# Stores to scratch memory on GpSimd's queue, loads and the final output on SyncE's

## The chip, the cores and the metric

The kernel runs on one core of a Trainium2 chip. The metric is the device time of one execution in microseconds (us), here the median of several. The engines of the core are TensorE (PE in the rows, PEld for its weight loads), VectorE (DVE), ScalarE (ACT), GpSimd (POOL) and SyncE (SP). Each works through its own instructions in order and waits for the others by semaphores. A transfer between the chip's memory and SBUF (a DMA) is issued as an instruction of one engine and then runs by itself. SPq in a row is SyncE's queue of such issues.

## What is computed

The reference is a trunk of two layers over 512 latent tokens and 256 context tokens, 1024 wide, in float32. Each layer modulates its input, projects it into three groups of heads (a state-space scan, latent attention, retention), gates each group, joins them, projects back and normalises:

```python
h_l = x * (1 + sc_l) + sh_l
parts_l = jnp.split(h_l @ w_in, in_splits(), axis=-1)
ssd_l, ssd_c = ssd_mixer(parts_c[0:3], parts_l[0:3], ...)
mla_l, mla_c = mla_mixer(parts_c[3:7], parts_l[3:7], ...)
ret_l, ret_c = retention_mixer(parts_c[7:11], parts_l[7:11], ...)
out_l = jnp.concatenate([ssd_l, mla_l, ret_l], -1) @ w_out
x_new = layer_norm(ALPHA * x + g_l * out_l, ln_g, ln_b)
```

The same is done for the context tokens (`_c`) in layer 0; in layer 1 only latent tokens go on. The latent attention first projects low-rank vectors into queries, keys and values, then attends with eight heads over all 768 tokens.

## The kernel before

Everything is held transposed, features on the 128 partitions and tokens along the row; 1024 features are eight tiles. A float32 product is made of three products of a reduced float32 format: ScalarE casts an operand to its high part (`wh` from the raw weight `wr`), VectorE subtracts it to get the low part (`wl`), and `mm3` (the helper around `mm`, L101) issues high x high, high x low and low x high. Raw weights of 512 KB come through two `wr` buffers, their two parts through three `wh` and `wl` buffers each. Outputs of a projection collect in accumulators named `pj` or `po`.

What does not fit in SBUF goes to scratch tiles in the chip's memory and is read back later, in every stage:

- `store` spills projections through a staging ring of three tiles `st`; `xbc` stores the convolved `xs`; `ssd_y` the scan's output `y`; `dt_stage` the small `kr` and `cum`.
- `ret_v` stages retention values in two buffers `stv` on the way to `rv`; `ret_y` stores the retention output to the scratch tiles `m4` to `m7`.
- `mla_prep` makes the attention's operands. All its results go through one ring of two buffers, tag `st`: the keys `kn` (four stores a layer), the values `v` (six, tile name `stv`), the queries `qh` (16). A buffer can be written again when its store has landed. Scores of one key head read `qr`, `kr` and `vr`, which are loaded back from `qh`, `kn`, `krr` and `v`; GpSimd's memsets (L991 to L994) fill the constant rows of those operands.
- `mla_head` normalises two heads at a time: the sums `den` are stored to `dd`, loaded back as `dc` spread over 128 partitions, inverted, stored to `de` and loaded back as `den`; then VectorE multiplies `num` by it and stores to `m0` to `m2`. This is done three times a layer.
- `out_s` runs half of the output projection beside the attention: it loads the residual `ox`, takes the accumulator `po` through VectorE's `oy`, adds, and stores to the scratch tile `a`. The loads `mraw` bring the retention output back, and ScalarE and VectorE split it into its two parts `mr`.
- `ln` stores the layer's output `x` and a row `rr`, to be read in the next layer.

Between these, `tick` spreads the modulation matmuls (`pr`, weights `ar`) over the program.

In the kernel before, all loads and all stores are `self.load`, that is `nc.sync.dma_start`, so SyncE issues them all, in one order. The order of each engine is set by a scheduler from the program's order, priorities (`high_priority` around the staging copies) and a cost of each instruction of its own.

Of the kernel before, what the change touches and what calls it, by code (L numbers as in the profile page):

```python
# [88 lines left out]
class Trunk:  # L89
# [7 lines left out]
    def load(self, out, in_):  # L97
        return self.nc.sync.dma_start(out=out, in_=in_)

# [331 lines left out]
    def dt_stage(self):  # L431
# [26 lines left out]
        self.load(D["kr"], ms[0:32, :])  # L458
# [50 lines left out]
        for d, m in ((0, self.mf), (1, self.mb)):  # L509
# [8 lines left out]
            self.load(D["cum"][d].rearrange("c h i -> h c i"), ct.rearrange("h (c i) -> h c i", i=128))  # L518
# [32 lines left out]
    def xbc(self, g):  # L551
# [8 lines left out]
        for t in range(4):  # L560
            u = self.conv(X_T + g * 4 + t)
            if self.ctx:
                self.load(D["xs"][g * 4 + t][:, 0:NCTX], u[:, 0:NCTX])
            self.load(D["xs"][g * 4 + t][:, NCTX:T], u[:, 260:XC])
# [42 lines left out]
    def ssd_y(self, c, g, hf, hb):  # L607
# [50 lines left out]
        self.load(D["y"][g][:, :, c * 128:(c + 1) * 128].rearrange("t p i -> p t i"), ys)  # L658


    def ret_v(self):
        l = self.l
        for n in range(2):
            sl = [self.wslot(self.A["win"][l, RV_T + n * 2 + j]) for j in range(2)]
            sl = [(a.rearrange("p (k c) -> p k c", k=4), b.rearrange("p (k c) -> p k c", k=4)) for a, b in sl]
            for c in range(NCH):
# [4 lines left out]
                with self.tc.high_priority():  # L671
# [9 lines left out]
                    self.load(self.D["rv"][:, c, n * 256:(n + 1) * 256], st)  # L681
# [145 lines left out]
    def ret_y(self, P, c0, q, kk, v, Dm, ef, hs):  # L827
# [44 lines left out]
        for s in range(2):  # L872
# [6 lines left out]
            for pr in range(2):  # L879
                self.load(D["m"][4 + pr * 2 + s][:, cs], gt[:, s, pr])  # L880


    def mla_prep(self, P):
# [47 lines left out]
        self.load(D["krr"], ko)  # L931
# [5 lines left out]
        for p in range(4):  # L937
# [7 lines left out]
            self.load(D["kn"][p], st)  # L945
        wvh, wvl = v3(wv[0], 2), v3(wv[1], 2)
        for c in range(NCH):
# [5 lines left out]
            self.load(D["v"][:, c, :], st)  # L953
# [3 lines left out]
        for s in (2, 0, 1):  # L957
            w = self.pslot(P, self.A["wuq"][l, s], 768)
            wh, wl = v3(w[0][:, 0:768], 3), v3(w[1][:, 0:768], 3)
            for j in range(2):  # L960
# [13 lines left out]
                if ti < 4:  # L974
                    for s2 in range(2):
                        self.load(D["qh"][ti * 2 + s2][0:64, lo:], st[64 * s2:64 * s2 + 64, lo:])
                else:
                    for s2 in range(4):
                        self.load(D["qh"][(ti - 4) * 4 + s2][64:96, lo:], st[32 * s2:32 * s2 + 32, lo:])
# [63 lines left out]
    def mla_head(self, P, h):  # L1043
# [37 lines left out]
        for i in range(2):  # L1081
            self.load(d1[i:i + 1, :], den[64 * i:64 * i + 1, lo:])
# [3 lines left out]
        self.load(fl(d2), dc)  # L1086
# [4 lines left out]
        self.load(D["m"][p][:, lo:], num[:, lo:])  # L1091
# [47 lines left out]
    def out_s(self, t):  # L1139
# [17 lines left out]
        self.load(self.D["a"][t][:, lo:], x[:, lo:])  # L1157
# [88 lines left out]
    def ln(self, P, X, a, b, qsum, xsum):  # L1246
# [32 lines left out]
        for t in range(8):  # L1279
# [5 lines left out]
            if a >= NCTX:  # L1285

                self.load(D["x"][t][:, a:b], X[t])
        if a >= NCTX:
            rr = P.tile([1, NLAT], F32, name="rr")
            self.copy(rr, pb[0:1, :])  # L1290
            self.load(self.rrd, rr)
# [91 lines left out]
```

## Time and profile before

| | us |
|---|---|
| median of 3 runs (1486.96 to 1489.88) | 1487.89 |
| the profiled execution | 1487.2 |
| its span | 1485.4 |
| TensorE busy (share of the span) | 1418.2 (95%) |
| VectorE busy | 1084.7 (73%) |
| ScalarE busy | 693.0 (47%) |
| GpSimd busy | 22.5 (2%) |

The profile records one execution. Its span runs from the first to the last instruction, and the rest of the execution's time, 1.8 us, lies around it. Issues of transfers, waits and register work are not counted as busy. A busy TensorE is not one at its peak, since matmuls overlap and their ends are modelled. A row such as "PE po <- DVE oy" tells that TensorE stood idle before the instruction that writes `po`, and that VectorE's instruction on `oy` ended the wait.

### The profile page before, as it was taken

The page shows a single profiled execution, that of the slowest core. Times are in us where ns is not written, and L with a number is a line of the kernel's source. Part 1 is how long each engine was busy: PE and PEld are TensorE (multiplying, and loading weights), DVE is VectorE, ACT ScalarE, POOL GpSimd, SP SyncE. Part 2 cuts the span into 40 slices and gives each one's busy share as a digit, 9 for nine tenths or more (in the row PEclk, how much of TensorE's full clock was granted, in tenths as well). Part 3 has the DMA queues.
Part 4 walks back from the last instruction along what each step waited for, and adds up shares of the span by engine and source line. Part 5 has one row for each costly group of instructions (what it writes and reads, how often), then busy time and mean ns, then how long its engine had stood idle before and what let it go on. Part 6 is the DMA issues. An engine that isn't in the chain of part 4 may idle for free. (4 is left out here: it accounts for less than half of the span.)

```text
span 1485.4 us, 23355 instructions
## 1 busy us (share of the span) xinstructions
PE 1418.2 (95%) x8660; PEld 1158.9 (78%) x8660; DVE 1084.7 (73%) x2132; ACT 693.0 (47%) x1376; POOL 22.5 (2%) x31
## 2 busy tenths in 40 slices
PE   6999999999999999999999799999999999989996
PEld 4787789778888878777788688789878887767665
DVE  3599894995485657678745858998697678678858
ACT  2346743662232434477721245565363335347743
POOL 0000000000000001000001000000000000000010
PEclk9999999999999999999999899999999999999998
DMA  8336543457724746724242222353257455563241
GB/s 335 137 101 178 184 171 107 158 183 256 256 72 157 254 160 182 240 65 137 89 156 71 91 88 87 129 135 114 86 171 226 173 188 189 196 202 98 67 128 57
DMA packets 110155, 225.66 MB, mean 152 GB/s; under 512 B 13581, under 2 KB 42381, under 8 KB 109786
## 3 DMA queue, kind: packets, MB, share of 16 engines
q1 hardware_dynamic: 110042, 224.17, 46.2%
q8 instruction: 68, 1.11, 0.3%
q14 instruction: 45, 0.37, 0.1%
HBM read 173.93 MB, written 50.20 MB: 151 GB/s over the span
## 5 line engine op out<-in xcount | busy, mean ns | idle before, releaser
L101 PE MATMUL pj<-hh,wh 128*128 128x512 f32 (+1 forms) x984 | 354.6, 361 | 2.0 <-ACT hh L115 1.6
L101 PE MATMUL pj<-hh,wl 128*128 128x512 f32 (+1 forms) x984 | 352.7, 359 | 0.0
L101 PE MATMUL pj<-hl,wh 128*128 128x512 f32 (+1 forms) x984 | 349.9, 356 | 0.0
L122 ACT CAST wh<-wr 128x1024 fp32r<-128x1024 f32 (+1 forms) x116 | 120.3, 1039 | 207.1 <-PE pj L101 94.0
L101 PEld LDWEIGHTS pj<-hh,wh 128*128 128x128 f32 x984 | 186.7, 190 | 34.0 <-issue 9.3
L101 PEld LDWEIGHTS pj<-hh,wl 128*128 128x128 f32 x984 | 186.4, 190 | 29.4 <-issue 7.0
L101 PEld LDWEIGHTS pj<-hl,wh 128*128 128x128 f32 x984 | 186.7, 190 | 29.0 <-issue 6.4
L104 DVE TENSOR_TENSOR wl<-wr,wh 128x1024 fp32r<-128x1024 f32 (+1 forms) x116 | 142.4, 1227 | 75.8 <-ACT wh L122 75.0
L104 DVE TENSOR_TENSOR pel<-pe,peh 128x512 fp32r<-128x512 f32 (+1 forms) x112 | 71.6, 648 | 35.8 <-ACT peh L115 35.3
L107 DVE SCALAR_TENSOR_TENSOR cv<-xpad,cw,cv 128x772 f32<-128x772 f32 (+1 forms) x96 | 92.2, 994 | 0.2
L115 ACT ACTIVATE pe<-psc 128x512 f32<-128x512 f32 (+1 forms) x112 | 63.7, 569 | 55.6 <-PE psc L101 46.7
L1035 DVE TENSOR_REDUCE nm<-pmx 128x1 fp32r<-128x768 f32 (+1 forms) x80 | 67.6, 845 | 15.8 <-PE pmx L101 14.6
L101 PE MATMUL po<-sh,wh 128*128 128x512 f32 (+1 forms) x192 | 69.4, 364 | 4.2 <-DVE oy L107 4.2
L101 PE MATMUL po<-sl,wh 128*128 128x512 f32 (+1 forms) x192 | 69.5, 363 | 1.7 <-DVE sl L107 1.7
L115 ACT ACTIVATE ce<-cf 64x512 f32<-64x512 f32 (+1 forms) x80 | 46.9, 586 | 49.6 <-DMA cf<-cum 48.9
L101 PE MATMUL po<-sh,wl 128*128 128x512 f32 (+1 forms) x192 | 68.9, 360 | 0.0
L115 ACT ACTIVATE tm<-sf,dt 128x128 f32<-128x128 f32 x160 | 52.5, 390 | 30.2 <-DVE sf L104 30.2
L115 ACT ACTIVATE peh<-psc 128x512 fp32r<-128x512 f32 (+1 forms) x112 | 63.6, 568 | 0.2
L115 ACT ACTIVATE arg<-arg,ncb 128x128 f32<-128x128 f32 x160 | 54.9, 393 | 4.2 <-DVE arg L107 3.8
L101 PE MATMUL pv<-wl,hh 128*128 128x256 f32 x192 | 54.7, 285 | 0.3 <-DVE wl L104 0.3
L101 PE MATMUL po<-mr,wh 128*128 128x256 f32 (+1 forms) x216 | 54.8, 339 | 0.0
L101 PE MATMUL pv<-wh,hl 128*128 128x256 f32 x192 | 54.5, 284 | 0.0
(330 smaller groups left out, 2952.2 us busy)
## 6 DMA issues: line engine op xcount, KB each, us to landing
wr<-in_win SPq DMA_DIRECT2D x82, 512.0 KB, 3.8
ar<-in_wada SPq DMA_DIRECT2D x48, 512.0 KB, 7.0
cf<-cum SPq DMA_DIRECT2D x80, 256.0 KB, 4.6
wr<-in_wout SPq DMA_DIRECT2D x32, 512.0 KB, 4.0
y<-ys SPq DMA_DIRECT2D x20, 256.0 KB, 2.6
xs<-th SPq DMA_DIRECT2D x16, 256.0 KB, 2.1
x<-in_xT SPq DMA_DIRECT2D x8, 384.0 KB, 8.7
rv<-stv SPq DMA_DIRECT2D x24, 128.0 KB, 2.6
```

The costliest lines, as they stand in the source:

```text
L101: return self.nc.tensor.matmul(out, lhsT=lhsT, rhs=rhs, start=start, stop=stop, **k)
L104: return self.nc.vector.tensor_tensor(out, a, b, op=op)
L107: return self.nc.vector.scalar_tensor_tensor(out, in0=a, scalar=s, in1=b, op0=op0, op1=op1)
L115: return self.nc.scalar.activation(out, in_, f, **k)
L122: self.nc.scalar.copy(hi, raw)
L1035: nc.vector.tensor_reduce(nm[:, i:i + 1], p1[:, 0:n], axis=AX.X, op=ALU.max, negate=True)
```

## The change

A new method `save` issues a transfer from GpSimd instead of SyncE, and every store to a scratch tile uses it: in `store`, `dt_stage`, `xbc`, `ssd_y`, `ret_v`, `ret_y`, `mla_prep`, `mla_head`, `out_s` and `ln`, some 230 stores. Loads and the store of the final output stay on SyncE. Source lines of the changed kernel are four higher (`mm` is L105 instead of L101).

```diff
     def load(self, out, in_):
         return self.nc.sync.dma_start(out=out, in_=in_)
 
+    def save(self, out, in_):
+
+        return self.nc.gpsimd.dma_start(out=out, in_=in_)
+
...
-            self.load(dst[:, ps[-1][1]:T], st[:, ps[-1][1]:T])
+            self.save(dst[:, ps[-1][1]:T], st[:, ps[-1][1]:T])
...
-                    self.load(self.D["rv"][:, c, n * 256:(n + 1) * 256], st)
+                    self.save(self.D["rv"][:, c, n * 256:(n + 1) * 256], st)
...
-            self.load(D["kn"][p], st)
+            self.save(D["kn"][p], st)
...
-            self.load(D["v"][:, c, :], st)
+            self.save(D["v"][:, c, :], st)
...
-                        self.load(D["qh"][ti * 2 + s2][0:64, lo:], st[64 * s2:64 * s2 + 64, lo:])
+                        self.save(D["qh"][ti * 2 + s2][0:64, lo:], st[64 * s2:64 * s2 + 64, lo:])
...
-            self.load(d1[i:i + 1, :], den[64 * i:64 * i + 1, lo:])
+            self.save(d1[i:i + 1, :], den[64 * i:64 * i + 1, lo:])
         dc = P.tile([128, k], F32, tag="dc", name="dc", bufs=2)
         self.load(dc, fl(d1))
         nc.vector.reciprocal(dc, dc)
-        self.load(fl(d2), dc)
+        self.save(fl(d2), dc)
...
-        self.load(self.D["a"][t][:, lo:], x[:, lo:])
+        self.save(self.D["a"][t][:, lo:], x[:, lo:])
```

The other stores are changed in the same way. Since the scheduler places every instruction anew, the order of the other engines changes in many small places too. Names below carry the number of the buffer.

SyncE, before, at the end of the query projections of layer 1 (`m5_1` to `m7_1` are retention scratch, `x3_0` is layer 0's output):

```order
L98 DMA mraw_13142<-m5_1_8742 128x512
L98 DMA qh2_1_8725<-st_12417 64x512
L98 DMA qh3_1_8726<-st_12417 64x512
L98 DMA qh4_1_8727<-st_12437 64x512
L98 DMA wr_14284<-in_wout 128x1024
L98 DMA qh5_1_8728<-st_12437 64x512
L98 DMA qh6_1_8729<-st_12451 64x512
L98 DMA qh7_1_8730<-st_12451 64x512
L98 DMA mraw_13146<-m6_1_8743 128x512
L98 DMA mraw_13150<-m7_1_8744 128x512
L98 DMA ox_14015<-x3_0_620 128x512
L98 DMA qr_12868<-qh0_1_8723 96x512
```

SyncE, after, the same place:

```order
L98 DMA wr_14140<-in_wout 128x1024
L98 DMA mraw_13138<-m4_1_8741 128x512
L98 DMA mraw_13142<-m5_1_8742 128x512
L98 DMA mraw_13146<-m6_1_8743 128x512
L98 DMA mraw_13150<-m7_1_8744 128x512
L98 DMA ox_14015<-x3_0_620 128x512
L98 DMA wr_14252<-in_wout 128x1024
L98 DMA ox_14054<-x4_0_621 128x512
L98 DMA qr_12868<-qh0_1_8723 96x512
```

The query stores have left this order, the four `mraw` loads stand next to each other, and `wr_14284` no longer stands ahead of the last two of them and of `qr`.

VectorE, before, where the first half of the output projection meets the start of attention in layer 1 (`st` are query stagings, `identr` a constant of the attention):

```order
L104 TENSOR_TENSOR wl_14143<-wr_14140,wh_14142 128x1024
L104 TENSOR_TENSOR mr11_12834<-mraw_13142,mr01_12830 128x512
L104 TENSOR_TENSOR st_12451<-pq_12452,nrb_12320 128x512
L104 TENSOR_TENSOR wl_14255<-wr_14252,wh_14254 128x1024
L984 CAST identr_12846<-K_72 128x128
L104 TENSOR_TENSOR mr12_12835<-mraw_13146,mr02_12831 128x512
L107 SCALAR_TENSOR_TENSOR oy_14016<-po_13990,mod1_77,rsb_12765 128x512
```

VectorE, after, the same place:

```order
L108 TENSOR_TENSOR wl_14104<-wr_14101,wh_14103 128x1024
L108 TENSOR_TENSOR mr12_12835<-mraw_13146,mr02_12831 128x512
L111 SCALAR_TENSOR_TENSOR oy_14016<-po_13990,mod1_77,rsb_12765 128x512
L108 TENSOR_TENSOR st_12451<-pq_12452,nrb_12320 128x512
L108 TENSOR_TENSOR mr13_12836<-mraw_13150,mr03_12832 128x512
L111 SCALAR_TENSOR_TENSOR ox_14015<-ox_14015,ag_552,rsb_12765 128x256
L111 SCALAR_TENSOR_TENSOR ox_14015<-ox_14015,ag_552,m3_12837 128x256
L111 SCALAR_TENSOR_TENSOR ox_14015<-ox_14015,ag_552,oy_14016 128x512
L111 SCALAR_TENSOR_TENSOR oy_14055<-po_14029,mod1_77,rsb_12765 128x512
L111 SCALAR_TENSOR_TENSOR ox_14054<-ox_14054,ag_552,rsb_12765 128x256
L108 TENSOR_TENSOR wl_14143<-wr_14140,wh_14142 128x1024
L988 CAST identr_12846<-K_72 128x128
```

`oy_14016` stood behind `wl_14255` and now stands ahead of `wl_14143`, which comes before that; `mr12` is ahead of it in both.

TensorE, before, at the start of attention in layer 0 (`pnm` turns the row maxima round, `pmx` are scores for maxima, `psc` scores):

```order
L101 MATMUL po_7541<-sh7_5885,wl_7513 128x256
L101 MATMUL pnm_6235<-identr_5962,nm_6212 1x128 x2
L101 MATMUL pnm_6239<-identr_5962,nm_6212 1x128 x4
L101 MATMUL pmx_6257<-bkh1_5976,bqh1_5974 128x256
L101 MATMUL psc_6292<-bqh0_5964,bkh0_5966 128x512
```

TensorE, after, the same place:

```order
L105 MATMUL po_7541<-sh7_5885,wl_7513 128x256
L105 MATMUL pnm_6235<-identr_5962,nm_6212 1x128 x2
L105 MATMUL pnm_6239<-identr_5962,nm_6212 1x128 x4
L105 MATMUL pr_7566<-ar_7567,sil_78 32x128 x8
L105 MATMUL pmx_6257<-bkh1_5976,bqh1_5974 128x256
L105 MATMUL psc_6292<-bqh0_5964,bkh0_5966 128x512
```

Eight modulation matmuls `pr` now stand between `pnm` and `pmx`.

## Rows read from the trace of the kernel before

**Rows 1.** The page: busy time, share of the span and instructions of each engine.

```profile
PE 1418.2 (95%) x8660; PEld 1158.9 (78%) x8660; DVE 1084.7 (73%) x2132; ACT 693.0 (47%) x1376; POOL 22.5 (2%) x31
```

**Rows 2.** What TensorE waited for: us in total, times, longest us.

```profile
PE prs L101 <- DVE rs_y L107: 10.5, 3, 4.7
...
PE po L101 <- DVE oy L107: 4.2, 2, 3.7
...
PE pq L101 <- ACT stv L115: 1.7, 1, 1.7
...
PE pvv L101 <- ACT stv L115: 1.3, 1, 1.3
```

**Rows 3.** What SyncE's queue waited for, same columns.

```profile
SPq L98 <- DVE wl L104: 239.6, 66, 12.1
...
SPq L98 <- ACT stv L115: 62.6, 35, 5.0
...
SPq L98 <- DVE ox L107: 46.6, 11, 21.1
```

**Rows 4.** Timeline of SyncE, layer 1: start, length, instruction, [idle before].

```profile
1300.47 0.34 SPq L98 DMA_DIRECT2D wr<-in_wout  x1
1300.87 1.92 SPq L98 DMA_DIRECT2D qh<-st  x3
...
1304.47 0.43 SPq L98 DMA_DIRECT2D qr<-qh  x1
...
1312.32 0.34 SPq L98 DMA_DIRECT2D a<-ox  x1
```

**Rows 5.** Timeline of VectorE, same place.

```profile
1306.77 1.23 DVE L104 TENSOR_TENSOR wl<-wr,wh 128x1024 fp32r<-128x1024 f32 x1 [5.12 <-ACT wh L122]
...
1308.77 0.75 DVE L107 SCALAR_TENSOR_TENSOR oy<-po,mod,rsb 128x512 f32<-128x512 f32 x1
```

**Rows 6.** Timeline of TensorE, start of attention, layer 0 and layer 1.

```profile
612.05 0.40 PE L101 MATMUL pnm<-identr,nm 128*1 128x128 f32 x4 [1.67 <-ACT bqh L118]
613.12 0.58 PE L101 MATMUL pmx<-bkh,bqh 96*128 96x256 f32 x1 [0.66 <-ACT bqh L118]
...
1309.57 0.79 PE L101 MATMUL po<-sh,wh 128*128 128x512 f32 x1 [3.69 <-DVE oy L107]
...
1325.14 0.40 PE L101 MATMUL psc<-bqh,bkh 97*128 97x512 f32 x1
```

**Rows 7.** Stretches: window, busy us and instructions by engine, granted clock, DMA share, GB/s.

```profile
610.00:620.00 10.00, 7.57 (x24) 5.16 (x25) 6.56 (x10) 4.72 (x8) 0.00 (x0) 0.66 0.75 270
...
1310.00:1320.00 10.00, 8.70 (x33) 6.47 (x33) 7.97 (x13) 4.06 (x6) 0.00 (x0) 0.87 0.80 238
```

**Rows 8.** The page, DMA issues: count, KB each, median us from issue to landing.

```profile
kn<-st SPq DMA_DIRECT2D x8, 384.0 KB, 2.3
v<-stv SPq DMA_DIRECT2D x12, 256.0 KB, 5.9
```

**Rows 9.** GpSimd's instructions by line: count, busy us, mean ns, idle before.

```profile
L1214 POOL TENSOR_TENSOR lxs<-lxs,la 128x512 f32<-128x512 f32 (+1 forms) x6 | 7.5, 1253 | 15.4 <-issue 10.3 <-DVE la L107 4.9
...
L991 POOL MEMSET bql<- 1x768 f32 x4 | 3.0, 741 | 677.8 <-DVE yg L104 677.7
```

**Rows 10.** What ScalarE waited for: us in total, times, longest us.

```profile
ACT stv L115 <- DMA rv<-stv: 6.4, 2, 3.7
...
ACT stv L115 <- DMA v<-stv: 5.1, 4, 1.8
```

**Rows 11.** What VectorE waited for, same columns.

```profile
DVE st L104 <- DMA qh<-st: 2.0, 2, 1.1
...
DVE num L107 <- DMA den<-de: 0.6, 1, 0.6
```

**Rows 12.** Timeline of SyncE, one of the six denominator chains.

```profile
725.60 0.32 SPq L98 DMA_DIRECT2D de<-dc  x1
727.00 1.09 SPq L98 DMA_DIRECT2D den<-de  x2
```

More of the change, by code (lines that the diff above doesn't have):

```diff
@@ L457, in dt_stage @@
                 self.padded[t] = self.pad(self.pre[t])
-        self.load(D["kr"], ms[0:32, :])
+        self.save(D["kr"], ms[0:32, :])
         pt = self.ps("tr", "pt", 2)
@@ L517, in dt_stage @@
             self.copy(ct[:, 512:T], pb[0:16, 0:256])
-            self.load(D["cum"][d].rearrange("c h i -> h c i"), ct.rearrange("h (c i) -> h c i", i=128))
+            self.save(D["cum"][d].rearrange("c h i -> h c i"), ct.rearrange("h (c i) -> h c i", i=128))
         self.cw = S.tile([128, 72], F32, name="cw")
@@ L562, in xbc @@
             if self.ctx:
-                self.load(D["xs"][g * 4 + t][:, 0:NCTX], u[:, 0:NCTX])
-            self.load(D["xs"][g * 4 + t][:, NCTX:T], u[:, 260:XC])
+                self.save(D["xs"][g * 4 + t][:, 0:NCTX], u[:, 0:NCTX])
+            self.save(D["xs"][g * 4 + t][:, NCTX:T], u[:, 260:XC])
             self.trans(u, self.xt[:, :, t * 128:(t + 1) * 128])
@@ L657, in ssd_y @@
         self.tt(yv, cv[hs[0][0]], py, ALU.add)
-        self.load(D["y"][g][:, :, c * 128:(c + 1) * 128].rearrange("t p i -> p t i"), ys)
+        self.save(D["y"][g][:, :, c * 128:(c + 1) * 128].rearrange("t p i -> p t i"), ys)
     def ret_v(self):
@@ L879, in ret_y @@
             for pr in range(2):
-                self.load(D["m"][4 + pr * 2 + s][:, cs], gt[:, s, pr])
+                self.save(D["m"][4 + pr * 2 + s][:, cs], gt[:, s, pr])
     def mla_prep(self, P):
@@ L930, in mla_prep @@
         nc.vector.tensor_copy(ko[:, 0:NCTX], kr[:, 0:NCTX])
-        self.load(D["krr"], ko)
+        self.save(D["krr"], ko)
         wk = self.pslot(P, self.A["wukv"][l, 0], 1024)
@@ L975, in mla_prep @@
                     for s2 in range(2):
-                        self.load(D["qh"][ti * 2 + s2][0:64, lo:], st[64 * s2:64 * s2 + 64, lo:])
+                        self.save(D["qh"][ti * 2 + s2][0:64, lo:], st[64 * s2:64 * s2 + 64, lo:])
                 else:
                     for s2 in range(4):
-                        self.load(D["qh"][(ti - 4) * 4 + s2][64:96, lo:], st[32 * s2:32 * s2 + 32, lo:])
+                        self.save(D["qh"][(ti - 4) * 4 + s2][64:96, lo:], st[32 * s2:32 * s2 + 32, lo:])
     def mla(self, P):
@@ L1090, in mla_head @@
         self.tt(num[:, lo:], num[:, lo:], gt[:, lo:], ALU.mult)
-        self.load(D["m"][p][:, lo:], num[:, lo:])
+        self.save(D["m"][p][:, lo:], num[:, lo:])
     def mla_last(self, P):
@@ L1285, in ln @@
             if a >= NCTX:
-                self.load(D["x"][t][:, a:b], X[t])
+                self.save(D["x"][t][:, a:b], X[t])
         if a >= NCTX:
@@ L1290, in ln @@
             self.copy(rr, pb[0:1, :])
-            self.load(self.rrd, rr)
+            self.save(self.rrd, rr)
 INS = ["xT", "cT", "wada", "win", "wuq", "wukv", "wout", "pc", "cpack", "rope"]
```

## The prediction

> **What bounds the kernel now.** The first view is the busy time of the engines [rows 1]: TensorE is busy for 95% of the span, so about 67 us of the 1485.4 are not matmul, and no change of queues can win more than a part of those. The second is the list of what TensorE waited for [rows 2]. Its largest entry is a chain of small VectorE operations, `rs_y`, that no store touches. The entries that a store can move are three: 4.2 us for `oy` (3.7 of it once), 1.7 and 1.3 us for `stv`, the staging tile of a store. The third view is what SyncE's queue waited for [rows 3]: it stood 239.6 us for `wl`, the release of a weight buffer, and 62.6 and 46.6 us for store sources, `stv` and `ox`. All of it is in program order, so a load behind a store waits until the store's source is written, and a store behind a weight load waits until that buffer is free. These long waits cost nothing where the loads run far enough ahead; the holes of TensorE tell where they do not.
>
> **The change, part by part.** The profiled execution took 1487.2 us, span 1485.4 and 1.8 around it; the median of the three runs is 1487.89, 0.7 us above it. The sum is made against 1487.2. A measurement of this kernel can tell about 0.2%, 3.0 us, so faster means below 1484.9 and slower above 1490.9.
>
> *The start of attention in layer 1.* Here TensorE has its one long hole that the change reaches: `po` starts at 1309.57 after 3.69 us without work, and waits for `oy` [rows 6]. `oy` frees the accumulator. On VectorE it stands behind `wl`, which starts at 1306.77 after 5.12 us for ScalarE's `wh` [rows 5], and that operand belongs to a weight that SyncE could only fetch at 1300.47, with three query stores behind it; the first head's query load follows at 1304.47 [rows 4]. The changed order takes all query stores out of SyncE and puts the four `mraw` loads in one block. As a result the scheduler places `oy` ahead of that `wl`: it now stands behind `mr12` instead. If nothing else is late, all 3.69 us go. What is next late is `mr12` itself, which needs a `mraw` load and a ScalarE cast, and one earlier weight operand. I take half, -1.85; ends -3.69 and 0.
>
> *The start of attention in layer 0.* Two holes, 1.67 and 0.66 us, both waiting for the cast `bqh` [rows 6]. The first stays: ScalarE's order before that cast is the same in both kernels, with a weight cast ahead of it. Ahead of the second, eight modulation matmuls (`pr`) now stand between `pnm` and `pmx`, which fill it: -0.66; ends -0.66 and 0.
>
> *The value stores of the latent attention.* The 12 stores `v<-stv` take 5.9 us from issue to landing where the larger `kn<-st` take 2.3 [rows 8], and with two staging buffers ScalarE waited 5.1 us in four places for them [rows 10]. Both of TensorE's holes behind `stv` [rows 2] come from this, 1.7 + 1.3 = 3.0 us. In before, such a store is issued into the same queue as the 512 KB weight loads. In a queue that holds stores alone it may land as `kn` does: -3.0. Or it lands as late as now and is issued later by GpSimd: the cost of that is not in the trace, since GpSimd issues no data there. Its lower bound is the 3.6 us (5.9 - 2.3) that a store can gain. For the upper I take the nearest work that GpSimd does: a memset of 741 ns and an addition of 1253 ns [rows 9], against 0.32 us for an issue on SyncE [rows 12], so +0.4 or +0.9 us a store. I take +0.4, the memset's, because it too is an instruction that reads nothing. For two places the ends are -3.0 and +1.9; I take half of the gain, -1.5.
>
> *The other staging rings.* ScalarE waited twice for `rv` stores (6.4 us) and VectorE twice for `qh` stores (2.0 us) [rows 10, 11], and none of these waits shows up in TensorE's list. Their cover is TensorE's own queue of matmuls of the next tile. With +0.4 us a store it holds: 0. Without cover it is 0.9 each, the rival's price below.
>
> *The denominators.* Six times in the program a pair of rows goes to scratch (`dd`), is read back spread over 128 partitions, inverted, stored (`de`) and read back. Between the issue of `de` at 725.60 and that of the load `den` at 727.00 lie 1.4 us [rows 12], and in one of the six VectorE waited 0.6 us for it [rows 11]; in the other five the data was there. So only that one has no slack, and its two store legs cost 2 x 0.4 = +0.8; ends 0 and, with all legs paid at 0.9, +11. The scheduler moves the multiplication that uses it one `pel` further back, which is cover for the rest.
>
> *What the stores are moved behind.* GpSimd had 31 instructions and 22.5 us of work [rows 1], so its queue has room; but it is in order too. In layer 1 the eight memsets of the attention operands now stand behind the store `a3`. That store was issued at 1312.32 in before [rows 4], eight memsets at 0.74 us make 5.9 [rows 9], so they would be done by 1318.6 with GpSimd's 0.4 for the store. They are first read by the scores `psc`, at 1325.14 [rows 6]. Cost 0, with 6.5 us to spare. Stores of `qh` now stand behind `a1` and `a2`, which wait for `ox`; the final loads need them no earlier than before. That some 230 stores leave SyncE's order is beyond doubt, so a change that does nothing is no rival.
>
> The sum: -1.85 - 0.66 - 1.5 + 0.8 = -3.2, so 1487.2 - 3.2 = **1484.0 us**.
>
> **The rivals.** *The holes close entirely.* All of 3.69, 0.66 and 3.0 go, 7.3 us, and with them the low clock behind two holes: in the ten microseconds from 610 and from 1310 TensorE was granted 0.66 and 0.87 of its 2.4 GHz [rows 7], between its two levels of 1.2 and 2.4 GHz, and had stood idle just before or inside both. 7.57 x 0.34 + 8.70 x 0.13 = 3.7 us of busy time can come back. 1487.2 - 7.3 - 3.7 = 1476.2. For it speaks that each hole has a store ahead of it on SyncE, against it that the 1.67 us hole of layer 0 is still there in the changed order.
>
> *Only the issue moves.* Stores and loads share the same transfer engines whoever issues them; a store that lands late because weight loads are moving still lands late, `mr12` takes the place of `wl` as what holds `oy`, and the time stays at 1487.2 + 0.8 - 0.66 = 1487.3: the same. The Trainium skill says this outright (DMA: Bandwidth & Descriptors, Issuing engines are not separate DMA queues): all DMAs end on the same 16 engines, and issuing from several saves only the issue time. By that sentence `v` would keep its 5.9 us; the trace of before has one queue only and cannot show it.
>
> *GpSimd's stores are late and the cover is gone*, which ends slower. The place is every ring of two buffers and the denominator legs: 2 + 4 + 2 waits that exist today [rows 10, 11] and six chains with one leg each that shows, 14 places. VectorE and ScalarE are in order, so what they owe TensorE (the `pel` operands and casts) waits with them. At +0.9 each that is 12.9, less the 2.5 of the two attention starts: 1487.2 + 10.4 = 1497.6. It decides from a store that lands 0.44 us later than now, where 14 x 0.44 - 2.5 reaches the 3.7 us that lie between 1487.2 and 1490.9. For it speaks that +0.4 is close to that point, against it that only two of the eight waits of today reach TensorE.
>
> *A store held up by VectorE's work.* VectorE is busy 73% [rows 1]. If certain of its operations keep GpSimd from issuing, a store can lose what separates the fast from the slow landing, 3.6 us [rows 8]. Two such hits on legs without slack make 1484.0 + 7.2 = 1491.2, slower. The Trainium skill describes this as a trap (SBUF — State Buffer, Who interferes with whom): copies and scalar operations in VectorE's two-port mode lock GpSimd out while it writes descriptors. By that rule only such operations count, and the VectorE rows around the attention starts are of other kinds; no run here shows the lock yet.
>
> **How the numbers follow.** The forecast 1484.0 gets 0.42; its own spread is about 3 us, since the order of VectorE, ScalarE and TensorE changes in many small places that I have not priced, so 0.24 of it lies below 1484.9 and 0.18 above. The holes that close entirely get 0.21 (faster), only the issue moves 0.11 (same), late stores 0.21 and held-up stores 0.05 (slower). Faster 0.24 + 0.21 = 0.45; same 0.18 + 0.11 = 0.29; slower 0.26. The range goes from 1476, the lower rival, to 1497, just inside the upper; what lies above it is the part of the late stores that cost more than 0.9 each, and below it more reordering than the holes hold, together 0.2. Faster and slower cases hold most of the chance; the likeliest one's own range is 1481 to 1487.
>
> **What would show it.** Right: after 1300 us `po` no longer waits 3.7 us for `oy`; the pair 1.67 and 0.66 becomes a single 1.7; `v<-stv` lands in under 4 us and TensorE's waits for `stv` are gone; `num` waits for `den` by about 1 us once, and its list of stores stands on GpSimd's queue. Wrong: `v<-stv` lands in 6 us or more, waits of ScalarE and VectorE for `qh`, `rv`, `dc` or `den` that are new and passed on to TensorE, or new holes at places that no store touches, which would be the reordering.

## The result, and the profile after

The changed kernel takes **1502.11 us** (median of four runs, 1499.77 to 1505.33); the kernel before, run beside it, 1488.89 (1486.96 to 1491.09). The ratio is **1.0094, 95% interval 1.0067 to 1.0122**: slower by 13 us, outside the range of the prediction and on its unlikely side. The profiled run took 1499.77 us with a span of 1498.0, against a span of 1485.4 before.

Lines of the page of the kernel after: busy time, share of the span and number of instructions of each engine, then the queues with packets, megabytes and share of the transfer engines' time. They answer to [rows 1]:

```profile
PE 1419.7 (95%) x8660; PEld 1160.5 (77%) x8660; DVE 1084.9 (72%) x2132; ACT 693.1 (46%) x1376; POOL 151.0 (10%) x262
...
q1 hardware_dynamic: 74016, 176.06, 36.7%
q0 software_dynamic: 14240, 48.12, 9.1%
```

The 48 MB of stores have a queue of their own, and GpSimd's busy time rose by 128 us: unlike SyncE's, GpSimd's issues count as busy on the page, 231 of them. TensorE's busy time grew by 1.5 us only, less than between two profiles of the kernel before (1418.2 and 1421.7, below). The loss is idle time of TensorE. The list of what it waited for (us in total, times, longest), answering to [rows 2]:

```profile
...
PE pvv L105 <- ACT stv L119: 5.9, 3, 3.9
PE pcol L105 <- DVE nx L108: 4.3, 3, 3.3
...
PE pnm L105 <- ACT bqh L122: 3.1, 1, 3.1
...
PE ppv L105 <- ACT peh L119: 2.8, 8, 1.2
PE pkn L105 <- DVE st L108: 2.1, 2, 1.7
PE pq L105 <- DVE st L108: 2.0, 1, 2.0
PE pkn L105 <- DVE pwl L108: 1.9, 1, 1.9
```

The entry for `oy` is gone, as forecast. The entries for `stv`, `st` and `nx` have grown or are new. Where the store and its staging copy stand in time in layer 0 is in three timelines of after: start, duration, engine, operation, and in brackets the idle time before it and what ended it. ScalarE and TensorE first, then the loads on SyncE, then the stores on GpSimd:

```profile
520.84 0.69 ACT L119 ACTIVATE stv<-pvv,rya 128x512 f32<-128x512 f32 x1 [3.07 <-PE pvv L105]
527.18 0.69 ACT L119 ACTIVATE stv<-pvv,rya 128x512 f32<-128x512 f32 x1 [5.65 <-DMA kn<-st]
...
527.92 0.50 PE L105 MATMUL pvv<-pwh,nh 128*128 128x512 f32 x1 [3.86 <-ACT stv L119]
...
515.12 0.33 SPq L98 DMA_DIRECT2D wr<-in_wout  x1
516.30 0.33 SPq L98 DMA_DIRECT2D ar<-in_wada  x1
...
519.05 0.33 SPq L98 DMA_DIRECT2D pwr<-in_wuq  x1
519.48 0.37 SPq L98 DMA_DIRECT2D ar<-in_wada  x1
...
519.60 0.54 POOL L102 DMA_DIRECT2D kn<-st  x1 [5.21 <-DVE st L108]
521.82 0.54 POOL L102 DMA_DIRECT2D v<-stv  x1 [1.68 <-ACT stv L119]
```

The last key store is issued at 519.60, after five loads, three of them 512 KB, that SyncE issued in the 4.5 us before it. The copy that needs its buffer starts at 527.18, 7.6 us later, where a key store took 2.3 us in the median before [rows 8]. TensorE has no free accumulator and stands 3.86 us. The medians alone would have misled: that of `v` improved, and that of `kn` rose by 0.4 us only. The list of DMA issues of after (count, size, median us to landing), answering to [rows 8]:

```profile
kn<-st POOLq DMA_DIRECT2D x8, 384.0 KB, 2.7
v<-stv POOLq DMA_DIRECT2D x12, 256.0 KB, 2.3
```

### The profile page after: what moved, and what is told of

It reads as the page before. It is cut to its first block, busy times and chain, and to the rows that moved or that the text cites. A ratio compares the mean times of both kernels' runs of the same rounds, so it can differ in the third digit from the quotient of the medians.

```text
span 1498.0 us, 23529 instructions
## 1 busy us (share of the span) xinstructions
PE 1419.7 (95%) x8660; PEld 1160.5 (77%) x8660; DVE 1084.9 (72%) x2132; ACT 693.1 (46%) x1376; POOL 151.0 (10%) x262
## 4 chain that ended last, share of the span: by engine, by line
PE 60%; issue 17%; DMA 8%; DVE 7%; ACT 6%; POOL 1%; SPq 0%; ACTq 0%; POOLq 0%; DVEq 0%
PE pj L105 22%; PE po L105 8%; PE ppv L105 5%; PE psc L105 4%; DMA cf<-cum 3%; PE pv L105 3%; PE pstate L105 2%; PE pq L105 2%; PE pr L105 2%; DVE cv L111 2%; PE pin L105 1%; PE pmx L105 1%; PE p L105 1%; PE py L105 1%; ACT wh L126 1%
## 5 line engine op out<-in xcount | busy, mean ns | idle before, releaser
L105 PE MATMUL pj<-hh,wh 128*128 128x512 f32 (+1 forms) x984 | 353.8, 360 | 2.0 <-ACT hh L119 1.6
L105 PE MATMUL pj<-hh,wl 128*128 128x512 f32 (+1 forms) x984 | 353.7, 360 | 0.0
L105 PE MATMUL pj<-hl,wh 128*128 128x512 f32 (+1 forms) x984 | 349.2, 355 | 0.0
L105 PEld LDWEIGHTS pj<-hh,wh 128*128 128x128 f32 x984 | 186.9, 190 | 34.3 <-issue 9.6
L105 PEld LDWEIGHTS pj<-hh,wl 128*128 128x128 f32 x984 | 186.3, 189 | 30.7 <-issue 8.3
L105 PEld LDWEIGHTS pj<-hl,wh 128*128 128x128 f32 x984 | 186.8, 190 | 27.6 <-issue 4.8
L105 PE MATMUL po<-sl,wh 128*128 128x512 f32 (+1 forms) x192 | 68.3, 360 | 0.7 <-DVE sl L111 0.7
L105 PE MATMUL po<-sh,wh 128*128 128x512 f32 (+1 forms) x192 | 68.8, 363 | 0.0
L105 PE MATMUL po<-sh,wl 128*128 128x512 f32 (+1 forms) x192 | 68.4, 357 | 0.0
L105 PE MATMUL po<-mr,wh 128*128 128x256 f32 (+1 forms) x216 | 55.1, 339 | 0.0
L105 PE MATMUL pv<-wl,hh 128*128 128x256 f32 x192 | 54.5, 284 | 0.3 <-DVE wl L108 0.3
L105 PE MATMUL pv<-wh,hh 128*128 128x256 f32 x192 | 54.6, 285 | 0.0
```

Of the source, the lines that this page charges most:

```text
L105: return self.nc.tensor.matmul(out, lhsT=lhsT, rhs=rhs, start=start, stop=stop, **k)
```

## The experiments

Two things change at once: the queue of some 230 stores, and, since the scheduler places everything anew, the order of every engine. All ratios are against the kernel before with 95% intervals. The indented texts are the expectations as recorded before each run; they call the kernels by labels, which are given here in brackets.

**Which stores.** The attention's preparation (`mla_prep`) holds the two-buffer ring. In the first kernel (e1) its stores go back to SyncE, as the cut shows; in the second (e2) they alone go to GpSimd.

```diff
-            self.save(D["kn"][p], st)
+            self.load(D["kn"][p], st)
...
-            self.save(D["v"][:, c, :], st)
+            self.load(D["v"][:, c, :], st)
```

> All of the change except mla_prep: its stores of krr, kn, v and qh go back to SyncE. Theory A (the operand stage mla_prep pays: the changed kernel is 12.5 us behind, 4.5 us of it collected by the start of attention in layer 0 and about 8 between 1190 and 1312 us, in layer 1's retention end and mla_prep): most comes back, 1491 to 1494 us. Theory B (stores from GpSimd cost a little everywhere, in all rings and denominators): about a third comes back, 1497 to 1499. Theory C (what costs is that the order of loads on SyncE changes once stores leave it, wherever they leave it): between these, and TensorE's holes before nx and pwl in layer 1 stay only if other stores are what moved the weight loads ahead.

> The kernel before with mla_prep's stores alone (krr, kn, v, qh) on GpSimd, all others on SyncE. Theory A: slower than before by 8 to 12 us, 1497 to 1501. Theory B: slower by 3 to 5. Theory C: slower by what the new order of loads inside mla_prep costs; holes of TensorE before nx, pkn and pvv as in the changed kernel.

Measured: 1.0098 [1.0076, 1.0120] and 1.0101 [1.0074, 1.0128]. Each half costs as much as the whole, so no sum over stores explains the loss, and theories A and B both miss. In the second the layer-0 hole behind `stv` is 3.72 us; in the first the list of TensorE's waits has no large `stv` entry, but 3.9 us for `nx` and 3.7 for `nm`. Both move the order, so neither settles anything.

**A third staging buffer** in the ring of `mla_prep` (tag `st`, 2 to 3), on after (e3) and on before (e4). If the ring is what waits, a third buffer should give it back.

```diff
-            st = P.tile([128, 512], F32, tag="st", name="stv5", bufs=2)
+            st = P.tile([128, 512], F32, tag="st", name="stv5", bufs=3)
```

> The changed kernel with three staging buffers instead of two in mla_prep, tag st. If the waits for landed stores (5.7 us of ScalarE for a kn store in layer 0, 3.2, 1.8 and 1.6 in layer 1) are what costs, the holes of TensorE behind stv and st (3.9 + 1.5 + 0.6 + 1.7 + 2.0 us) close and the time falls by 7 to 10 us, to 1492 to 1495. Theory C: the load of nx behind a weight load remains (a hole of 3.3 us) and the bqh one of 3.1, and the time falls by 3 or less, 1499 or more.

> The kernel before, all on SyncE, with three staging buffers in mla_prep. The control of the run above: TensorE's holes behind stv and st there are 1.7 + 1.3 + 0.6 us, so 0 to 3.5 us faster than before, 1485 to 1489. If it gains as much as the third buffer does in the changed kernel, the ring is not what the change made worse.

Measured: 1.0315 [1.0283, 1.0347] and 1.0082 [1.0056, 1.0108]. The buffer costs time even where all stores stay on SyncE: the scheduler makes another order with it. So the test says nothing on the ring. It hints that a new order alone can cost 0.8%; the buffer changed with it.

**Queue and order apart.** The program is built twice. The first build only yields an order; in the second each instruction is tied, without a wait, to the one that stood before it on its engine in the first. A kernel with an order kept in this way is called pinned below. So the first kernel (p1) has before's order row for row, with only the issuer of the stores changed; the second (p2) has after's order with all stores merged back into SyncE's queue.

```diff
+    POOLQ = False
...
+    def save(self, out, in_):
+        return (self.nc.gpsimd if Trunk.POOLQ else self.nc.sync).dma_start(out=out, in_=in_)
...
+            for i in sorted((i for i in traced if i.name in rank), key=lambda i: rank[i.name]):
+                e = str(i.engine)
+                if e in last:
+                    tc.add_manual_dep(i, last[e].name, mybir.DependencyInfo(
+                        mybir.DependencyClass.NoSync, mybir.DependencyReason.DATA), reason="pin")
+                last[e] = i
```

> The order of the kernel before is kept on every engine, row for row; only the scratch stores are issued by GpSimd instead of SyncE, in the order they had. So this is the queue without the new order. Theory O (the loss of the change is its new order of instructions; all of e1, e2, e3 and e4 moved the order and all lost 12 us or more): within 4 us of before, or faster by the 1 to 3 us that the value stores and freed loads were forecast to give, a ratio of 0.997 to 1.003. Theory Q (late stores from GpSimd): 1498 us or more, a ratio of 1.007 or more.

> The order of the changed kernel is kept on every engine; all scratch stores go back to SyncE, merged among its loads as the scheduler dated them. So this is the new order without the new queue. Theory O: as slow as the changed kernel or slower, ratio 1.008 or more, since the stores now also hold up loads. Theory Q: within 4 us of before, ratio 0.997 to 1.003.

| | stores on SyncE | stores on GpSimd |
|---|---|---|
| order of before | 1 | 1.0097 [1.0078, 1.0117] |
| order of after | 1.0096 [1.0075, 1.0118] | 1.0094 [1.0067, 1.0122] |

**Either part alone costs the whole 0.95%**, and together they cost no more. So there are two causes, each of which is enough. The order's part is seen in TensorE's waits with the order of after and all stores on SyncE:

```profile
PE pvv L107 <- ACT stv L121: 4.2, 3, 2.6
...
PE pcol L107 <- DVE nx L110: 4.0, 2, 3.1
...
PE ppv L107 <- ACT peh L121: 2.8, 8, 1.2
...
PE pkn L107 <- DVE pwl L110: 2.1, 1, 2.1
...
PE pkn L107 <- DVE st L110: 1.6, 2, 1.4
```

These are entries that are new or larger in after, without any store on GpSimd: `nx`, `peh` and `pwl` with nearly the same sizes, `stv` and `st` smaller. One of them can be followed in after. In layer 1 the two loads `nx<-ckv` (the first rows that the attention normalises) stood back to back in before; now a weight load stands between them. SyncE and TensorE of after:

```profile
1228.86 0.43 SPq L98 DMA_DIRECT2D nx<-ckv  x1
1232.69 0.33 SPq L98 DMA_DIRECT2D wr<-in_wout  x1
1233.12 0.38 SPq L98 DMA_DIRECT2D nx<-ckv  x1
...
1242.21 2.38 PE L105 MATMUL pcol<-ones,nx 128*128 128x1 f32 x12 [3.33 <-DVE nx L108]
```

The weight load waits for its buffer, the second `nx` waits behind it, and what is computed from it is late. That ScalarE's and VectorE's own new orders add to it is likely, and was not tested. The kernel with after's order and all stores on SyncE has the same three loads in the same sequence.

To see how far any change of order hurts, one step of layer 1's plan is swapped in the kernel before, all stores on SyncE (n1; a small change, some 40 rows on four engines stand elsewhere):

```diff
-         "dt0 xbc0 rk1 ssd0 rk0 xbc1 rv0 ssd1 ckv1 ckv0 cq0 cq1 rg0 rg1 rg2 rg3 cq2 g0 g1 g2 g3")
+         "dt0 xbc0 rk1 ssd0 rk0 xbc1 rv0 ssd1 ckv1 ckv0 cq0 cq1 rg0 rg1 rg2 rg3 g0 cq2 g1 g2 g3")
```

> The kernel before, all on SyncE, with two projections of layer 1 in the other order in the table of steps (cq2 g0 becomes g0 cq2). The work is the same; it is a sample of what an order other than the kept one costs. Theory O: slower, by 3 to 15 us. Theory Q: within 3 us of before.

Measured: 0.9998 [0.9980, 1.0016]. So not every new order costs, though this one is small beside after's.

**Whose queue.** With the order of before pinned, only the 36 value stores (`v` and `rv`) leave SyncE, once for ScalarE (p7) and once for GpSimd (p8). Theory H is that loads which run ahead of a store make it land late, theory G that an issue from GpSimd does.

```diff
+    def save2(self, out, in_):
+        return (self.nc.scalar if Trunk.POOLQ else self.nc.sync).dma_start(out=out, in_=in_)
...
-            self.load(D["v"][:, c, :], st)
+            self.save2(D["v"][:, c, :], st)
```

> The order of the kernel before; only the 36 stores that ScalarE's own results feed (v and rv) leave SyncE, and they are issued by ScalarE right behind the instruction that writes them. A queue of its own, but not GpSimd's. Theory H: loads run ahead here too, and it loses 3 to 6 us like p8. Theory G: within 2 us of before.

> The same 36 stores on GpSimd instead. In p1 TensorE's holes behind stv are 4.5 us in layer 0 where before has 1.7. Both theories: 3 to 6 us slower than before; H says as much as p7, G says 2 us or more slower than p7.

Measured: 1.0068 [1.0043, 1.0093] and 1.0071 [1.0048, 1.0094]; the hole behind `stv` in layer 0 is 4.55 and 4.34 us. Both lose some 10 us, more than the 3 to 6 expected. GpSimd is no worse than ScalarE, so for these stores neither its price of an issue nor a lock by VectorE is the cause. It is enough that the store has a queue of its own.

**Why the store lands late.** Before and the pinned kernel with stores on GpSimd have the same order, so their rows can be laid side by side. SyncE, ScalarE and TensorE of before at the value stage of layer 0:

```profile
521.95 1.49 SPq L98 DMA_DIRECT2D v<-stv  x2
523.53 0.89 SPq L98 DMA_DIRECT2D ar<-in_wada  x2
525.61 1.33 SPq L98 DMA_DIRECT2D v<-stv  x2
...
524.89 0.69 ACT L115 ACTIVATE stv<-pvv,rya 128x512 f32<-128x512 f32 x1 [1.80 <-DMA v<-stv]
...
532.93 0.50 PE L101 MATMUL pq<-nh,pwh 128*128 128x512 f32 x1 [1.70 <-ACT stv L115]
```

The pinned kernel, SyncE, GpSimd, ScalarE and TensorE:

```profile
524.81 0.83 SPq L100 DMA_DIRECT2D ar<-in_wada  x2
...
526.76 0.54 POOL L104 DMA_DIRECT2D v<-stv  x1 [5.05 <-ACT stv L121]
527.93 0.54 POOL L104 DMA_DIRECT2D v<-stv  x1 [0.63 <-ACT stv L121]
...
534.11 1.48 ACT L121 ACTIVATE stv<-pvv,rya 128x512 f32<-128x512 f32 x2 [6.48 <-DMA v<-stv]
...
534.85 0.79 PE L107 MATMUL pvv<-pwh,nh 128*128 128x512 f32 x1 [4.46 <-ACT stv L121]
```

In before the two 512 KB modulation loads `ar` stand behind the first two value stores and cannot start until these are issued. The third copy gets its buffer 2.9 us after the first store's issue (521.95 to 524.89). With the stores on another queue nothing holds the `ar` loads: they start 1.95 us ahead of the first store, and its buffer comes free 7.3 us after its issue (526.76 to 534.11). TensorE does not stand at the third copy in before; its hole of 1.70 us in layer 0 comes later, at the fifth copy, which waits for the third store. That store is issued at 525.61 behind the `ar` loads, and its buffer comes free 6.6 us later, at 532.18. In the pinned kernel the transfer engines are nearly full in that stretch. The windows of the pinned kernel (us; busy time and instructions of PE, PEld, DVE, ACT, POOL; TensorE's granted clock; share of the transfer engines; GB/s):

```profile
524.00:528.00 4.00, 4.00 (x19) 3.24 (x18) 1.55 (x4) 2.22 (x3) 0.61 (x2) 1.00 0.94 332
528.00:532.00 4.00, 2.39 (x11) 1.60 (x9) 1.02 (x1) 0.00 (x0) 0.47 (x1) 1.00 0.97 299
532.00:536.00 4.00, 1.15 (x3) 0.96 (x4) 0.00 (x0) 1.38 (x2) 0.66 (x2) 0.79 0.43 172
```

So the theory was: **the old store order was also a brake on the loads, and the second queue removes it.** The full engines alone don't tell the kernels apart: in before their share is 0.96 from 523 to 527 us (the row is in the last section), but there the first two stores are ahead of the loads. If the theory holds, one queue must show the same hole if only those two loads are moved ahead of the first two value stores (p10), and a kernel with the loads moved behind the fourth store (p12) should lose the hole that before has. In the cuts `k0`, `k2`, `k3` and `k4` are the places of the first to fourth value store of layer 0. Before itself was run again (c0; its edit only adds a method that nothing calls).

```diff
+            early = [n for n in order[k2:k3] if n in Trunk.AR]
+            order = [n for n in order[:k0] if n not in early] + early + [n for n in order[k0:] if n not in early]
```

```diff
+            late = [n for n in order[k2:k3] if n in Trunk.AR]
+            order = [n for n in order[:k4 + 1] if n not in late] + late + order[k4 + 1:]
```

> The kernel before, everything on SyncE and in the same order, but for one swap: in layer 0 the two modulation loads ar (512 KB each) that stood behind the first two value stores v stand ahead of them. Theory H: the stores land late with no second queue at all; TensorE's hole behind stv there grows from 1.7 to 3.5 us or more, and the time by 2 to 4 us, 1490 to 1493 against 1488 to 1491 of before. Theory G: no change, the hole stays near 1.7.

> The opposite swap of p10_ar_ahead: the kernel before, with the two modulation loads ar behind the fourth value store of layer 0 instead of behind the second. Theory H: stores 3 and 4 find the transfer engines free as well, the hole behind stv (1.7 us in before) goes, and the time is 0 to 3 us below before, a ratio of 0.998 to 1.000; slower by 1 to 3 if the modulation matmuls then wait for ar.

> The kernel before once more (every store called by its own method, all on SyncE; the instructions and their order are the same). A second profile of the same program: how much of a difference between two profiles is only from one execution to the next. Ratio 0.998 to 1.002; the moments of the weight operands in layer 1 within 2 us of the first profile's if the drift of 5 us seen there with p10_ar_ahead is the swap's, 3 us or more apart if it is not.

Measured: 1.0039 [1.0015, 1.0064] for the loads ahead, 1.0002 [0.9988, 1.0016] for the loads behind, and 0.9990 [0.9974, 1.0007] for before. The kernel with the loads behind is pinned, so pinning by itself costs nothing that shows. The loads ahead, all on SyncE:

```profile
519.37 0.86 SPq L100 DMA_DIRECT2D ar<-in_wada  x2
521.07 8.95 SPq L104 DMA_DIRECT2D v<-stv  x4
...
528.37 1.30 ACT L121 ACTIVATE stv<-pvv,rya 128x512 f32<-128x512 f32 x2 [6.15 <-DMA v<-stv]
...
529.11 0.79 PE L107 MATMUL pvv<-pwh,nh 128*128 128x512 f32 x1 [4.15 <-ACT stv L121]
```

The swap of two loads on one queue makes nearly the same wait (6.15 against 6.48) and hole (4.15 against 4.46), and the time rises by 6 us, where 2 to 4 were expected. A part of this is lost in layer 1. By the mark set for before's second profile it belongs to the swap: the `po` behind `oy` starts at 1309.57 and 1309.98 in before's two and at 1318.40 here. How two loads in layer 0 do that was not followed. With the loads behind, the hole behind `stv` in layer 0 is gone, and the time is the same: a hole of 1.1 to 1.7 us is too small to show.

The counter-test (p9) keeps the stores on GpSimd, and lets the load that follows a value store in the old order wait until that store has landed:

```diff
+                if i.name in Trunk.V:
+                    held = i.name
+                elif "SP" in e and held is not None:
+                    tc.add_manual_dep(i, held, mybir.DependencyInfo(
+                        mybir.DependencyClass.Sync, mybir.DependencyReason.DATA), reason="land")
+                    held = None
```

> As p1_old_order_pool (order of before, all stores on GpSimd), and in mla_prep the next load on SyncE behind a value store waits until that store has landed. Theory H (a store on its own queue shares the transfer engines with loads issued ahead of their old place): in layer 0 TensorE's hole behind stv, 4.5 us in p1, falls to 1.7 or less, and ScalarE's wait of 6.5 to under 3; the time falls by 3 to 6 us against p1, to 1499 to 1503. Theory G (landing from GpSimd is late by itself): the hole stays above 3.5, and the time is p1's or more.

Measured: 1.0051 [1.0030, 1.0071], against 1.0097 [1.0078, 1.0117] without the hold: some 7 of the 14 us come back, and `stv` falls in TensorE's list to 0.6 us in all. So the wait and the hole are shown to come from the loads. That the 7 us come from closing this hole is not shown. The first value copy of layer 0, where nothing has been held yet, starts 8 us apart in the two profiles (without the hold, with it):

```profile
525.78 0.69 ACT L121 ACTIVATE stv<-pvv,rya 128x512 f32<-128x512 f32 x1 [0.56 <-PE pvv L107]
...
517.82 0.69 ACT L121 ACTIVATE stv<-pvv,rya 128x512 f32<-128x512 f32 x1 [0.55 <-PE pvv L107]
```

From there to the end of the span both take 978 us, and before's second profile takes 970. So in these two executions the hold gains nothing from that point on; with it TensorE has new holes of 1.34 us (`nx`, layer 0) and 2.40 us (`rya`, layer 1).

The hold also explains the `nx` entry of the pinned kernel (2.8 us, layer 1). It is the same mechanism, with ScalarE as the carrier. ScalarE and TensorE there, without the hold:

```profile
1283.19 0.69 ACT L121 ACTIVATE stv<-pvv,rya 128x512 f32<-128x512 f32 x1 [2.58 <-DMA v<-stv]
1283.77 1.14 ACT L121 ACTIVATE nx<-nx 128x512 f32<-128x512 f32 x2
...
1285.97 1.87 PE L107 MATMUL pcol<-ones,nx 128*128 128x1 f32 x8 [2.75 <-DVE nx L110]
```

and ScalarE with the hold:

```profile
1275.82 0.69 ACT L121 ACTIVATE stv<-pvv,rya 128x512 f32<-128x512 f32 x1
1276.41 1.14 ACT L121 ACTIVATE nx<-nx 128x512 f32<-128x512 f32 x2
```

The sixth value copy waits 2.58 us for a store, and the squares of `nx` stand behind it on ScalarE. TensorE's list names `nx`, but what is late is again a value store. With the hold TensorE does not wait there.

**Giving the brake back everywhere.** A weaker hold (p6) puts back only what one queue does: a load waits for the instruction that writes the source of the store ahead of it. The next (p13) adds the wait for landing for all stores of `mla_prep`; the last (p14) does the same with the order of after.

```diff
+                if "SP" in e and HOLD and not_yet:
+                    for w in not_yet:
+                        tc.add_manual_dep(i, w, mybir.DependencyInfo(
+                            mybir.DependencyClass.Sync, mybir.DependencyReason.DATA), reason="hold")
+                    not_yet.clear()
+                if i.name in source:
+                    not_yet.add(source[i.name])
```

```diff
-                    not_yet.add(source[i.name])
+                    not_yet.add(i.name if i.name in Trunk.PREP else source[i.name])
```

> As p1_old_order_pool (the order of the kernel before, stores issued by GpSimd), and each load on SyncE that stood behind a store there now waits for the instruction that writes that store's source, as it did when the store stood ahead of it in SyncE's queue. Theory H (what a store on SyncE did besides storing was to hold back the loads behind it; on its own queue it meets 512 KB loads that were issued early, and shares the transfer engines with them): at least half of p1's 14 us come back, 1492 to 1499 us, and in layer 0 ScalarE's wait of 6.5 us for a v store falls under 3. Theory G (the issue from GpSimd itself makes stores land late): no change against p1, 1503 us or more.

> p6_hold and p9_v_landed together: the order of before, all scratch stores on GpSimd; loads on SyncE that stood behind a store wait for its source as in p6, and in mla_prep for the landing of kn, v, krr and qh. Theory H accounts for all of p1's loss: within 4 us of before, ratio 1.003 or less. If a part belongs to GpSimd's issue itself: 1.005 or more, as p6 and p9.

> The changed kernel, its own order row for row, with the same holds as p13. Theory H: the loads that run ahead are also what costs in the changed kernel's own order: half of its 13 us or more come back, ratio 1.005 or less, and the hole of 3.9 us behind stv in layer 0 falls under 2. If the changed kernel's loss is its order, nothing comes back: 1.008 or more.

Measured: 1.0061 [1.0039, 1.0083], 1.0095 [1.0074, 1.0116], 1.0170 [1.0138, 1.0201]. The first gives back some third of the loss, where theory H asked for half, and the intervals with and without the hold overlap; the layer-0 hole is 2.44 us, and ScalarE still waits 3.48 us for a value store, where under 3 was expected. The other two give nothing back, and theory H misses in both. Their holds make loads late as well: TensorE's list of p13 has 2.2 us for the weight operand `pwh` and 1.2 us for the load `rvt`, which the pinned kernel has at 0.5 and not at all. So they don't decide between the theories, and no hold reaches before.

**The account.** Waits of TensorE in us by what ended them, from the profile of each run; the last waits row is the sum over the whole list. "Queue" and "order" are the two pinned kernels, "held" and "swap" the counter-test and the two loads ahead on one queue.

| | before | before again | after | order | queue | held | swap |
|---|---|---|---|---|---|---|---|
| `stv` (for `pvv`, `pq`) | 3.0 | 3.1 | 5.9 | 4.2 | 4.7 | 0.6 | 6.1 |
| `nx` (for `pcol`) | 0.0 | 0.2 | 4.3 | 4.0 | 2.8 | 1.3 | 0.4 |
| `st` (for `pkn`, `pq`) | 0.8 | 1.5 | 4.1 | 3.0 | 0.9 | 2.5 | 1.5 |
| `peh` (for `ppv`) | 1.2 | 1.1 | 2.8 | 2.8 | 1.1 | 1.2 | 1.2 |
| `pwl` (for `pkn`) | 1.1 | 1.0 | 1.9 | 2.1 | 1.0 | 1.1 | 1.0 |
| `oy` (for `po`) | 4.2 | 4.2 | 0.0 | 0.0 | 4.2 | 4.2 | 4.4 |
| all waits | 57.4 | 58.2 | 68.9 | 68.0 | 67.0 | 62.4 | 64.3 |
| TensorE busy | 1418.2 | 1421.7 | 1419.7 | 1422.0 | 1427.2 | 1424.0 | 1422.5 |
| span | 1485.4 | 1489.5 | 1498.0 | 1499.8 | 1504.0 | 1496.1 | 1496.2 |

After against before: 11.5 us of the 12.6 in the span are waits of TensorE. Against before's second profile the waits grow by 10.7 us and the span by 8.5. The 1.3 us of `nx` that are left with the hold are in layer 0.

## Why the prediction was wrong

**The start of attention in layer 1 (forecast -1.85).** The mechanism was right and the term too small: `oy` is gone from the list, where it had 4.2 us, 3.7 of them the hole of [rows 6]. With before's order pinned the `oy` wait stays at 4.2, so it was the order that removed it, as the prediction had it.

**The start of attention in layer 0 (-0.66).** The second hole did not go: `pr` stands in it, but waits 0.56 us for its own load `ar`. And the first grew from 1.67 to 3.11, where the prediction had it stay. ScalarE's order ahead of `bqh` is the same, as the prediction read it, but a cast of `mr` in it starts late, at 613.61 after 4.03 us for its load `mraw`. This belongs to the order: with after's order and all stores on SyncE the hole is 2.40 us, with before's order and the stores on GpSimd 1.09. TensorE of after, answering to [rows 6]:

```profile
616.56 0.59 PE L105 MATMUL pnm<-identr,nm 128*1 128x128 f32 x4 [3.11 <-ACT bqh L122]
617.71 1.08 PE L105 MATMUL pr<-ar,sil 128*32 128x128 f32 x16 [0.56 <-DMA ar<-in_wada]
```

**The value stores (-1.5) are the step that failed.** Its premise was that a store in a queue of stores alone may land as `kn` does. It took the landing time for a property of the queue. The runs show that it depends on which loads were let go before it: 7.3 us instead of 2.9 with the same order, and the same on one queue with two loads moved. The bounds were built on the median of twelve stores, and that median did fall to 2.3 us while TensorE's wait behind `stv` rose from 3.0 to 5.9. A few stores met bursts of loads, and these were the ones waited for: the twelve `v` stores of after landed in 2.3 us in the median and 6.5 at most, the eight `kn` in 2.7 and 7.5. The upper end, +1.9 for two places, came from the issue price alone. A bound for a late landing stood in the rows that the prediction read: value stores already took 5.9 us in the median [rows 8], with `ar` loads beside some of them. The 3.6 us between that and `kn` was taken as what a store can gain; it should have stood as what one can lose as well, at each place. The statement of the Trainium skill (DMA: Bandwidth & Descriptors, Issuing engines are not separate DMA queues) that transfers of all issuers end on the same 16 engines and interleave fits these rows, with 0.94 to 0.97 of the engines' time in the windows above. Its second sentence, that a second issuer saves only the time to issue, is true of what is saved; the runs add what is lost, the order between the queues.

**GpSimd's issue (+0.4 us a store)** was about twice what it is. The issue of a value store takes 0.54 us on GpSimd against 0.32 on SyncE [rows 12], +0.22. It did not decide: with an issue of 0.33 us from ScalarE the 36 stores cost as much, within the intervals.

**The denominators (+0.8) and the memsets (0).** VectorE's wait for `den` rose from 0.6 to 1.4 us, the +0.8 forecast, but in two places, and TensorE's list shows nothing of its size, so that the number agrees is luck. The memsets end at 1325.7, not at 1318.6, since the stores ahead of them on GpSimd were issued up to 1320.4; nothing waits for them: the first `pmx` (1328.76) waits 0.57 us for ScalarE's cast `bkh`.

**The rivals.** "Late stores, cover gone" gave 1497.6 and came nearest, and its sign was right, but not its reason: it had each store cost by its issue, at 14 places (14 x 0.9 is 12.6, not the 12.9 of its sum), and the point of decision at +0.44 us. What happened is few stores late by over 4 us. "Only the issue moves" (the same time) and "the holes close entirely" fell. "Held up by VectorE" (Trainium skill, SBUF — State Buffer, Who interferes with whom) found no support: the same loss comes with ScalarE as the issuer of the 36 value stores, and the twelve `v` stores of after take 0.539 to 0.548 us each to issue, so none was held up while it was issued. One of VectorE's rows at the start of attention in layer 1, the cast `identr`, is of the kind that the prediction found absent there.

**The order was not priced**, and the prediction said so, but gave it a spread of 3 us. It is worth 0.96% by itself. Of after's waits it brings nearly all of `nx`, `peh` and `pwl` and most of `st`; against before's second profile all waits grow by 9.8 us, although `oy` loses its 4.2. That the two causes don't add is measured; why is only partly read. They meet at the same places (`stv`, `nx`), where the longer wait may hide the shorter; this is argued, not shown.

**Open.** The mechanism of a late store is shown; what it is worth in time is not. The pinned kernel with the stores on GpSimd loses 14.5 us. The hold for value stores takes 7 off the median, but the profiles don't place them, and the kernel with 36 stores on GpSimd has its hole of 4.34 us in a profiled execution whose span, 1490.7 us, is only 1.2 above before's second profile, while the median of its six runs lies 10 us above before. The pinned kernel's profile also has a busy time 5.5 us above before's second profile, at a mean granted clock of 0.976 against 0.980. Two profiles of the kernel before differ by 4.1 us in span, and the pinned kernel and the one with the hold by 8 before they do anything different, so pieces of this size can't be assigned one by one.

## What to carry to other kernels

A store in a load queue can also be a brake: before it is moved to a queue of its own, look at which large loads stand behind it and whether a two-buffer ring waits for its landing, since these loads will be let go ahead of it. Where a scheduler rebuilds the order, pin the old order once and change one thing, or the two effects can't be told apart; a new order alone cost 0.96% here, and another, smaller one nothing. A median landing time says nothing on the one landing that is waited for: read the row of the wait.

## What the runs showed of the hardware

A 256 KB store's buffer came free 2.9 us after its issue with two 512 KB loads issued after it and 7.3 us with the same loads issued 2 us ahead, from two queues and, with 1.7 us ahead, from one. The issue of such a store took 0.54 us on GpSimd, 0.32 on SyncE and 0.33 on ScalarE; the difference between GpSimd and ScalarE was not seen in the time. The hole of 4 us was followed by a lower granted clock: in the kernel with the two loads ahead on one queue (first two windows, columns as above) it was 1.00 in the stretch where the hole began and 0.65 in the next, between TensorE's two levels of 1.2 and 2.4 GHz. In before (last two windows), where TensorE works through the same stretch, it stayed at 1.00.

```profile
523.00:527.00 4.00, 1.97 (x9) 1.28 (x7) 1.02 (x1) 0.00 (x0) 0.00 (x0) 1.00 0.81 296
527.00:531.00 4.00, 1.89 (x5) 1.50 (x6) 0.00 (x0) 1.30 (x2) 0.00 (x0) 0.65 0.42 162
...
523.00:527.00 4.00, 4.00 (x19) 3.12 (x18) 1.02 (x1) 1.48 (x3) 0.00 (x0) 1.00 0.96 311
527.00:531.00 4.00, 4.00 (x19) 3.09 (x17) 2.23 (x3) 2.61 (x3) 0.00 (x0) 1.00 0.89 308
```

So a hole can cost more than its length, in before as well [rows 7]; how much more by the end of the program was not measured.
